# Moving the scatters of many-counted rows forward in the Pool queue of an argmax, gather and scatter kernel

## The chip, the cores and the metric

One core of a Trainium2 chip runs the whole kernel. The metric is the device time of one execution in microseconds (us). The profile's span is some 2 us shorter than the device time, because it starts and ends with the instructions.

## The reference, cut to what matters

```python
B, S, H = (8, 2048, 2560)
best_j = np.argmax(scores, axis=2)            # for each of 2048 rows of a batch, one chosen row
gathered = values[b_idx, best_j, :]
out = np.zeros_like(values)
np.add.at(out, (b_idx, best_j, slice(None)), gathered)
```

So an output row is zero if nobody chose it, a copy of the row of `values` if it was chosen once, and that row times its count if it was chosen more often. A row has 10,240 bytes.

## The kernel before

VectorE finds the argmax of each score row, matmuls count the choices, and three lists are made per batch: rows chosen once, never, and many times. The GpSimd (Pool) queue then moves the rows by indirect DMA, 128 rows ("a column") at a time; rows of a column that are not on its list are skipped.

- `copy_once(t)`: values to output in DRAM, the single rows of column t.
- `scatter(zrow, zi)`: zeros to the output.
- `gather` into one of six staging slots in SBUF, ScalarE multiplies by the count, `scatter` to the output. A slot can be filled again only when its scatter has landed.

```python
        def gathers():
            for k in range(MCAP):                     # 5 columns
                v = stage()                           # next of NV = 6 slots
                gather(v, mi[:, k:k + 1])
                nc.scalar.activation(out=v, in_=v, func=..., scale=mc[:, k:k + 1])
                staged.append(v)
                if rest:
                    copy_once(rest.pop(0))

        def zeros():
            for k in range(ZLAST if b == B - 1 else ZCAP):    # 12 or 7 columns
                scatter(zrow[:], zi[:, k:k + 1], free_running)
                if rest:
                    copy_once(rest.pop(0))

        if b == 0:
            zeros()
            # ... ten steps of the next batch's counting ...
            gathers()
        else:
            gathers()
            zeros()
        for k in range(MCAP):
            scatter(staged[k], mi[:, k:k + 1])
```

The rows of a column are spread over the 16 DMA engines, and by chance of the input some engines get fewer single rows than others. For the last batch, `level_engines` counts each engine's rows of the whole kernel and hands out the last 746 zero rows so that all engines come to nearly the same total: the lightest two engines get 76 zero rows each, the heaviest 20.

## Time and profile before

| | before |
|---|---|
| median of the first three runs | 840.63 us (839.85 to 841.81) |
| span of the profiled run | 838.4 us |
| DMA busy share, slices 1 to 39 of 40 | 0.9 or more in each |
| VectorE / Pool busy | 81% / 33% |
| rows moved by the Pool queue | 20,762, that is 212.6 MB |

The DMA row of the page says what bounds the kernel: 16 engines that are nearly never idle. In this view the last two columns are the mean busy share of the 16 DMA engines and GB/s.

```profile
632.00:637.00 5.00, 0.00 (x0) 0.00 (x0) 4.97 (x4) 0.00 (x0) 2.00 (x2) 1.00 0.94 377
696.00:701.00 5.00, 0.05 (x2) 0.00 (x0) 1.01 (x10) 0.00 (x0) 2.21 (x3) 1.00 0.94 383
760.00:764.00 4.00, 0.00 (x0) 0.00 (x0) 0.00 (x0) 0.00 (x0) 1.99 (x2) 1.00 0.98 405
```

Full is about 1.01 or 1.02 here, since a packet starts a few ns before the previous one ends.

### The profile page before, as it was taken

How to read it: one execution, taken by the hardware profiler on the slowest of the kernel's cores; microseconds unless marked ns; L12 is line 12 of the kernel's file. 1: busy time of each engine (PE TensorE's matmuls, PEld its weight loads, DVE VectorE, ACT ScalarE, POOL GpSimd, SP SyncE). 2: the span in 40 equal slices, each digit the busy share in tenths (PEclk: the TensorE clock that was granted, in tenths of full speed). 3: DMA queues.
4: the chain of work that ended last, by engine and by line, in shares of the span. 5: the costliest groups of instructions: out<-in, count | busy, mean ns of one | idle time of the engine just before them, and what ended most of it. 6: DMA issues, size and time to landing. Idle time of an engine off the chain costs nothing.

```text
span 838.4 us, 2053 instructions
## 1 busy us (share of the span) xinstructions
PE 14.7 (2%) x273; PEld 14.1 (2%) x273; DVE 678.6 (81%) x794; ACT 102.9 (12%) x43; POOL 274.3 (33%) x277
## 2 busy tenths in 40 slices
PE   0000000000000000000000000000000000000000
PEld 0000000000000000000000000000000000000000
DVE  7999999999999999999999999999999992000000
ACT  2000001401300002200003200013100500500500
POOL 0000743267101254130263300551305724734720
DMA  9999999999999999999999999999999999999992
GB/s 383 426 429 431 380 421 422 421 407 428 422 431 426 425 427 431 426 426 427 427 428 428 428 427 425 429 425 427 427 426 409 420 425 412 417 416 418 418 418 117
DMA packets 48111, 347.04 MB, mean 414 GB/s; under 512 B 19014, under 2 KB 19014, under 8 KB 19014
## 3 DMA queue, kind: packets, MB, share of 16 engines
q0 software_dynamic: 38736, 212.67, 61.4%
q1 hardware_dynamic: 9360, 134.22, 37.6%
q14 instruction: 13, 0.11, 0.0%
q8 instruction: 2, 0.03, 0.0%
HBM read 354.42 MB, written 300.15 MB: 781 GB/s over the span
## 4 chain that ended last, share of the span: by engine, by line
DVE 69%; DMA 12%; POOL 5%; issue 4%; another core or an unknown queue 4%; ACT 0%; PE 0%; POOLq 0%
DVE am L185 32%; DVE mx L184 29%; DMA out_dram<-vbig,many_i 9%; DMA vbig<-in_values_dram,many_i 3%; POOL out_dram L151 2%; DVE oh_lo L194 2%; POOL out_dram L33 2%; DVE oh L321 2%; POOL vbig L146 1%; DVE lo L190 1%; DMA vbig<-in_scores_dram 1%; DVE oh_hi L198 0%; ACT vbig L359 0%; DVE put L336 0%
## 5 line engine op out<-in xcount | busy, mean ns | idle before, releaser
L185 DVE FIND_INDEX8 am<-mx,s_tile 128x8 uint32<-128x2048 f32 x116 | 265.0, 2285 | 0.0
L184 DVE MAX8 mx<-s_tile 128x8 f32<-128x2048 f32 x116 | 264.3, 2278 | 0.0
L33 POOL DMA_INDIRECT out_dram<-in_values_dram,ones_i x128 | 131.2, 1025 | 157.1 <-DVE m L292 119.0
L359 ACT ACTIVATE vbig<-vbig,many_c 128x2560 f32<-128x2560 f32 x40 | 96.7, 2426 | 693.8 <-DMA vbig<-in_values_dram,many_i 693.8
L146 POOL DMA_INDIRECT vbig<-in_values_dram,many_i x40 | 42.4, 1060 | 230.2 <-DMA out_dram<-vbig,many_i 182.3
L151 POOL DMA_INDIRECT out_dram<-vbig,many_i x40 | 38.9, 972 | 122.5 <-ACT vbig L359 118.0
L151 POOL DMA_INDIRECT out_dram<-zrow,zero_i x61 | 60.6, 994 | 18.9 <-issue 18.9
L184 DVE MAX8 mx<-vbig 128x8 f32<-128x2048 f32 x12 | 27.4, 2279 | 4.8 <-DMA vbig<-in_scores_dram 4.8
L185 DVE FIND_INDEX8 am<-mx,vbig 128x8 uint32<-128x2048 f32 x12 | 27.4, 2285 | 0.0
L194 DVE TENSOR_TENSOR oh_lo<-lo,lane_f 128x512 bf16<-128x512 uint32 x32 | 22.2, 693 | 0.4
L321 DVE TENSOR_TENSOR oh<-lo,fill_f 128x2048 f16<-128x2048 uint32 x8 | 18.3, 2291 | 0.3
L203 PE MATMUL cnt_ps<-oh_hi,oh_lo 128*128 128x16 bf16 x128 | 8.1, 174 | 578.3 <-DVE oh_hi L198 578.3
L203 PEld LDWEIGHTS <-oh_lo 128*128 128x128 bf16 x128 | 8.4, 105 | 578.1 <-DVE oh_lo L194 577.1
L185 DVE MATCH_VALUE_LOAD am<-mx,s_tile 128x8 f32 x116 | 10.7, 92 | 4.0
L198 DVE TENSOR_TENSOR oh_hi<-hi,lane_f 128x64 bf16<-128x64 uint32 x32 | 6.9, 217 | 0.0
L190 DVE TENSOR_SCALAR lo<-am 128x4 uint32<-128x4 uint32 x32 | 5.8, 183 | 1.1
L339 PE MATMUL l_ps<-put,oh 128*128 128x32 f16 x128 | 4.7, 188 | 68.5 <-DVE put L336 68.5
L339 PEld LDWEIGHTS <-oh 128*128 128x128 f16 x128 | 4.6, 104 | 69.6 <-DVE oh L321 59.2
L192 DVE TENSOR_SCALAR hi<-am 128x4 uint32<-128x4 uint32 x32 | 5.5, 172 | 0.0
L326 DVE TENSOR_TENSOR ez<-hi,lane_f 128x256 f16<-128x256 uint32 x8 | 3.3, 418 | 0.0
L336 DVE TENSOR_TENSOR put<-ez,row_f 128x256 f16<-128x256 f16 x8 | 3.3, 417 | 0.0
L347 DVE TENSOR_SCALAR e<-l_ps 128x32 f32<-128x32 f32 x8 | 1.5, 185 | 2.0 <-PE l_ps L339 2.0
(91 smaller groups left out, 60.3 us busy)
## 6 DMA issues: line engine op xcount, KB each, us to landing
s_tile<-in_scores_dram SPq DMA_DIRECT2D x58, 2048.0 KB, 12.0
vbig<-in_scores_dram SPq DMA_DIRECT2D x5, 2048.0 KB, 32.6
vbig<-in_scores_dram SPq DMA_DIRECT2D x2, 1024.0 KB, 6.1
out_dram<-in_values_dram,ones_i POOLq DMA_INDIRECT x128, 28.3
out_dram<-zrow,zero_i POOLq DMA_INDIRECT x61, 25.4
vbig<-in_values_dram,many_i POOLq DMA_INDIRECT x40, 32.3
out_dram<-vbig,many_i POOLq DMA_INDIRECT x40, 46.4
```

The lines of the kernel that those rows point to most:

```text
L33: return eng.add_instruction(ins)
L146: nc.gpsimd.indirect_dma_start(out=v, out_offset=None, in_=values_flat[:, :], in_offset=bass.IndirectOffsetOnAxis(ap=idx, axis=0), bounds_ ...
L151: note(nc.gpsimd.indirect_dma_start(out=out_flat[:, :], out_offset=bass.IndirectOffsetOnAxis(ap=idx, axis=0), in_=v, in_offset=None, bound ...
L184: nc.vector.max(out=mx[:], in_=rows)
L185: nc.vector.max_index(out=am[:, g, :], in_max=mx[:], in_values=rows)
L190: nc.vector.tensor_single_scalar(out=lo[:], in_=am[:, :, 0], scalar=P - 1, op=ALU.bitwise_and)
L194: nc.vector.tensor_tensor(out=oh_lo[:], in0=lo[:].unsqueeze(2).to_broadcast([P, G, P]), in1=lane_f[:].unsqueeze(1).to_broadcast([P, G, P]) ...
L198: nc.vector.tensor_tensor(out=oh_hi[:], in0=hi[:].unsqueeze(2).to_broadcast([P, G, NT]), in1=lane_f[:, 0:NT].unsqueeze(1).to_broadcast([P, ...
L203: nc.tensor.matmul(out=cnt_ps[:], lhsT=oh_lo[:, g, :], rhs=oh_hi[:, g, :], start=(t == 0), stop=(t == NT - 1))
L321: nc.vector.tensor_tensor(out=oh[:], in0=lo[:].unsqueeze(2).to_broadcast([P, NT, P]), in1=fill_f[:].unsqueeze(1).to_broadcast([P, NT, P]), ...
L339: nc.tensor.matmul(out=l_ps[:], lhsT=oh[:, t, :], rhs=put[:, t, :], start=(t == 0), stop=(t == NT - 1))
L359: nc.scalar.activation(out=v, in_=v, func=mybir.ActivationFunctionType.Copy, bias=0.0, scale=mc[:, k:k + 1])
```

## The change

The intent: a batch's scatters go out earlier, so its staging slots come free earlier and the next batch's gathers wait less. No instruction is added or removed.

```diff
+    ZHEAD = 4
...
-        def zeros():
-            for k in range(ZLAST if b == B - 1 else ZCAP):
+        def zeros(columns):
+            for k in columns:
...
+        nz = ZLAST if b == B - 1 else ZCAP
         if b == 0:
-            zeros()
+            zeros(range(nz))
...
         else:
             gathers()
-            zeros()
+            zeros(range(ZHEAD))
         for k in range(MCAP):
             scatter(staged[k], mi[:, k:k + 1])
+        if b > 0:
+            zeros(range(ZHEAD, nz))
+        assert not rest
         yield
```

In batches 2 to 6 three zero columns and three copy columns go behind the scatters, in batch 7 eight and three. In batch 1 it is three and one, because that batch starts with six copy columns and not four.

## The prediction

> **What bounds the kernel now.** I read the page's second part (the 40 slices) first, then the DMA queues, the waits, the stretches of the tail, and last the Pool queue in order of time.
>
> ```profile
> span 838.4 us, 2053 instructions
> ...
> DVE  7999999999999999999999999999999992000000
> ...
> POOL 0000743267101254130263300551305724734720
> DMA  9999999999999999999999999999999999999992
> ...
> q0 software_dynamic: 38736, 212.67, 61.4%
> q1 hardware_dynamic: 9360, 134.22, 37.6%
> ```
>
> The DMA row is full in 39 of 40 slices, while Pool, the engine whose order changes, is busy a third of the time and VectorE has nothing left after about 697 us. q0 is the Pool queue (copies, zeros, gathers, scatters), q1 the score loads: 61.4 + 37.6 = 99% of the 16 engines' span. The chain of waits puts 69% on VectorE; I do not take that as the bound, since the same chain is then followed through DMA for its last 240 us and the DMA row has no hole under the VectorE part either.
>
> ```profile
> POOL vbig L146 <- DMA out_dram<-vbig,many_i: 182.3, 19, 41.5
> ...
> POOL out_dram L151 <- ACT vbig L359: 118.0, 25, 9.9
> ```
>
> These two waits (total, times, longest) are what the change acts on: a gather waits until the previous batch's scatter has left its staging slot, and a scatter waits until ScalarE has multiplied a gathered tile. They look large, 300 us, but Pool can wait as long as its queue still holds transfers. Whether it does is read from the stretches (the last two columns are DMA share and GB/s):
>
> ```profile
> 630.00:640.00 10.00, 0.00 (x0) 0.00 (x0) 9.93 (x7) 0.00 (x0) 4.17 (x5) 1.00 0.98 398
> 690.00:700.00 10.00, 0.59 (x16) 0.58 (x16) 6.11 (x25) 0.00 (x0) 1.51 (x2) 1.00 0.97 404
> 750.00:760.00 10.00, 0.00 (x0) 0.00 (x0) 0.00 (x0) 0.00 (x0) 0.00 (x0) 1.00 1.02 422
> 810.00:820.00 10.00, 0.00 (x0) 0.00 (x0) 0.00 (x0) 0.00 (x0) 0.00 (x0) 1.00 0.97 403
> 820.00:830.00 10.00, 0.00 (x0) 0.00 (x0) 0.00 (x0) 0.00 (x0) 0.00 (x0) 1.00 0.36 149
> ```
>
> From 750 to 760 Pool does nothing and DMA still moves 422 GB/s. After Pool's last issue (ends at 803.55 us) the transfers go on until about 829.6 in the packet records, then some 9 us of closing work follow. So the end is set by the bytes.
>
> **What the Trainium skill says.** "DMA: Bandwidth & Descriptors", section "Queues, rings and completion order": each of the 16 engines takes a ring's descriptors in order and goes round-robin between the queues. Its section "Anatomy of one DMA — SWDGE (gpsimd) path" says that DMA engines never wait on semaphores, the issuing sequencer does. Both agree with the trace: the gather issued at 770.59 landed at 795.06, 24 us behind older work. Section "Why a DMA increments its semaphore by 16 and not by 1": a transfer counts as landed when the slowest engine has; I use that for the tail. "Perfetto Trace Analysis", section "Per-instruction lifecycle": the profiled time of a Pool DMA is descriptor generation, not movement; the trace agrees, 0.96 us shown for a scatter against a median of 46.4 us to landing.
>
> **The change part by part.** It removes and adds no instruction. In batches 1 to 7 three zero columns (eight in the last batch) and three single-row copies go behind the five scatters. One issue takes 1.28 us (0.98 busy, 0.30 issue).
>
> Sizes: the reference's draw is fixed, so I counted rows. Over all batches 6131 are never chosen, 5875 once, 4378 more often; with gather and scatter that is 6131 + 5875 + 2 x 4378 = 20762 rows of 10,240 B = 212.6 MB, which is q0's size. Batch 7 has 746, 757 and 545. A full column (128 rows, 1.31 MB) takes 3.1 us at the tail's 418 GB/s; a copy column (47 rows) 1.15 us.
>
> *A middle boundary, batch 6 to 7, in the tail's rate.* The zeros start at 710.77. Now four zeros and four copies (8 x 1.28 = 10.2 us) end at 721.0, where the first scatter stands instead of at 728.73. Multiplies end at 717.25, 721.42, 725.67, 731.01 and 733.33, so the scatters go out near 721.0, 722.3, 726.0, 731.3 and 733.6, that is 7.7, 7.7, 5.3, 1.3 and 0.3 us earlier. Only the early ones gain; the last was bound by its gather. The six issues behind take Pool to 742.3. The transfers moved are 1.83 zero columns (5.7 us) and three copies (3.4 us), 9.1 us no longer ahead of the first scatter, which lands near 752 instead of 761. The first gather that reuses a slot then waits about 2 us where it waited 18.87:
>
> ```profile
> 741.56 0.99 POOL L33 DMA_INDIRECT out_dram<-in_values_dram,ones_i  x1 [0.30 <-issue]
> 761.43 1.01 POOL L146 DMA_INDIRECT vbig<-in_values_dram,many_i  x1 [18.87 <-DMA out_dram<-vbig,many_i]
> ```
>
> The columns are start, busy time, the instruction, and its idle time with the releaser. That is 17 us of Pool's time, and I expect next to nothing of it in the span: that gather still has all of batch 6 ahead of it in the same ring, in another order, so with a ring that never empties it lands when it landed before. What it can win is the dips: 630 to 640 moved 398 GB/s and 690 to 700 moved 404, against about 427 around them. That is 10 x 29/427 + 10 x 23/427 = 1.2 us in all. The moved columns lie just where these dips begin, so I count half to all: **-0.6 to -1.2 us**.
>
> *The last batch.* Gathers are issued by about 763, four zeros and their copies by 775. Its multiplies end where they ended:
>
> ```profile
> 792.40 2.43 ACT L359 ACTIVATE vbig<-vbig,many_c 128x2560 f32<-128x2560 f32 x1 [1.06 <-DMA vbig<-in_values_dram,many_i]
> 795.09 2.43 ACT L359 ACTIVATE vbig<-vbig,many_c 128x2560 f32<-128x2560 f32 x1 [0.27 <-DMA vbig<-in_values_dram,many_i]
> ```
>
> So Pool stands at the scatters from 775 until 797.5, where it waited 0.3 us before, and then issues eight zeros and three copies: 11 x 1.28 = 14.1 us, ending near 812.6 instead of 803.55. **Pool ends 9 us later.** Is that hidden? Behind the last gather, on the slowest engine at 795, still lie five copies and four zero columns, about 5.8 + 8 to 12 us, and four scatters of 3.1 us, over 26 us together; it reaches 821 without anything issued after 795. So the latest engine has no hole. The leveling of the last batch, worked out from the same counts, gives one engine 20 zero rows and the lightest 76. The lightest has almost no backlog at 775: nine columns issued there last it 18 us from 763, to about 781, and the scatters come to it at 783, 786.8, 791.4, 794.9 and 797.5 with 3.1 us each. It stands idle perhaps 3 to 5 us; then 44 zero rows and some 9 copied rows of 0.39 us take it to about 820, still ahead of the 829.6 of the latest. Cost **0, at worst +4 us**.
>
> Sum: 840.63 - 0.9 + about 0.3 for a small chance of the worst = **840.0 us**.
>
> **The rivals.** (1) *The early slot wins:* Pool's 182 us of slot waits shrink and the span with them. For it: Pool is at the end of the chain. Against it: DMA was full during those waits. Even if it won all dips and half of the uneven end (829.6 against some 822 if all engines ended together), that is 5 us: 835.5. (2) *A new wait takes its place:* Pool stands at the scatters (118 us of waits grow to perhaps 180) with nine issued columns behind the last gather instead of fifteen, the ring runs dry, and what is dry is lost. For it: after 618 us there are no score loads to fill in. Against it: 18 us of work are still behind the last gather. If it happened on the latest engine in the last two batches, some 5 us each: 850. (3) *Pool becomes the bound of the tail:* 14 us of issue for 10 us of rows (267 zero rows and 3 x 47 copies at 0.0245 us). Against it: the scatters' 13 us are still queued when it begins; perhaps +2 us.
>
> **Range and chances.** The median I expect is **840.0 us**, 8 times in 10 between **836.5** and **844.5**: the lower end is about four fifths of rival 1, the upper half of rival 2; runs of the kernel before already spread over 2 us. Over 2% would be 17 us. Faster by that is more than dips and uneven end hold together, chance **0.02**; slower needs the ring dry for 17 us, **0.03**; within 2% **0.95**.
>
> **What would show it.** Pool's slot waits fall well below 182 us, its waits for ScalarE rise well above 118, both without effect. DMA stays at 1.0 between 740 and 815; the dip near 635 is shallower. Pool's last issue falls near 812, its wait before the last batch's scatters sums to some 15 to 20 us. The multiplies of batch 7 still start near 780 to 795. I would be wrong if stretches with DMA share under 0.95 appeared before 810 (rival 2), or if the multiplies of batch 7 came several us earlier (rival 1).

## The result, and the profile after

| | before | after |
|---|---|---|
| median, six runs each | 840.62 us | 835.80 us (835.43 to 836.25) |
| ratio | | 0.9942 (0.9929 to 0.9955) |
| span | 838.4 us | 834.0 us |
| last row landed (packet records) | 829.65 us | 824.58 us |

Ratios here and below are the mean time of one kernel's runs over that of the other's in the same rounds, so they differ a little from the ratio of the medians. The change is 0.6% faster, and its 835.80 us lies just under the predicted 836.5 to 844.5.

The same rows of the page after:

```profile
span 834.0 us, 2053 instructions
...
POOL 0000642256021250071410422501516167266260
DMA  9999999999999999999999999999999999999993
...
q0 software_dynamic: 38736, 212.67, 61.5%
q1 hardware_dynamic: 9360, 134.22, 37.9%
```

The bytes are the same; 38,736 and 9,360 packets as before. The waits after (total, times, longest):

```profile
POOL out_dram L152 <- ACT vbig L360: 236.5, 39, 24.7
...
POOL vbig L147 <- DMA out_dram<-vbig,many_i: 83.6, 16, 21.1
```

Pool waits 99 us less for slots and 118 us more for multiplied tiles: it waits longer in all, and the kernel is faster. The sum of Pool's waits says nothing about the time. The stretches do:

```profile
632.00:637.00 5.00, 0.00 (x0) 0.00 (x0) 4.97 (x5) 0.00 (x0) 3.24 (x4) 1.00 1.02 420
696.00:701.00 5.00, 0.59 (x16) 0.48 (x15) 1.52 (x12) 0.00 (x0) 3.82 (x4) 1.00 1.01 422
...
820.00:830.00 10.00, 0.00 (x0) 0.00 (x0) 0.00 (x0) 0.00 (x0) 0.00 (x0) 1.00 0.15 51
```

Both dips are full again, and in 820 to 830 us the share is 0.15 where it was 0.36: the engines stop more nearly together. The Pool queue in order of time and ScalarE's last batch (start, busy, instruction, idle before it and releaser) show that the main times of the prediction came true:

```profile
752.13 1.01 POOL L147 DMA_INDIRECT vbig<-in_values_dram,many_i  x1 [1.97 <-DMA out_dram<-vbig,many_i]
...
781.70 0.98 POOL L152 DMA_INDIRECT out_dram<-vbig,many_i  x1 [7.67 <-ACT vbig L360]
785.52 0.97 POOL L152 DMA_INDIRECT out_dram<-vbig,many_i  x1 [2.84 <-ACT vbig L360]
...
810.33 0.96 POOL L152 DMA_INDIRECT out_dram<-zrow,zero_i  x1 [0.30 <-issue]
```

```profile
779.00 2.43 ACT L360 ACTIVATE vbig<-vbig,many_c 128x2560 f32<-128x2560 f32 x1 [45.53 <-DMA vbig<-in_values_dram,many_i]
```

The first reused slot was free at 752.13 after a wait of 1.97 us (predicted: 752, 2 us), Pool's last issue ended at 811.3 (predicted 812.6), and the last batch's multiplies began 1.5 us earlier. Not all of it fitted: Pool began the zeros of batch 6 at 701.59 and not at 710.77, because the boundary before it had changed too, and then stood 6.09 us at the first scatter. Yet the last row landed 5.1 us earlier.

**Which engines ended last.** The trace records each DMA packet with start, length and size, without its engine. On one engine a packet starts 3 to 4 ns before the previous ends, a row takes 385 ns and a skipped row appears as a 4-byte packet of 9 ns. Which rows each engine moves, in which order, follows from the reference's fixed input and from the spread of partitions over engines: for transfers from SBUF that of the Trainium skill, "DMA: Bandwidth & Descriptors", section "The descriptor swizzle", engine = 8 x (p >> 6) + ((p >> 2) & 7); for DRAM to DRAM p >> 3, as the kernel's own leveling assumes. I searched the packet records backwards for each engine's known sequence of rows and skips. Before, all 16 were found, over 220 or more consecutive packets each; after, 14. So this trace agrees with that page's mapping. The end of each engine's last packet, with its zero rows of the last batch:

```
engine (zero rows)   before    after
 0 (24)              819.2     818.8
 1 (21)              819.3     820.5
 3 (20)              825.7     824.2      <- heaviest
 4 (35)              824.7     824.2
11 (64)              827.1     820.5
 8 (59)              827.4     824.2
 9 (76)              829.6     823.7      <- lightest
12 (76)              829.6     824.6      <- lightest
```

Before, the **lightest** engines ended last, four microseconds behind the heaviest. The leveling gave them the most zero rows at the end in the belief that they had a lead; they had lost that lead earlier by standing idle, and by rows that took longer than the others (both below).

Linking the packets into 16 chains without any knowledge of the engine, and counting after 622 us: before, gaps of over 50 ns sum to 17.1 engine-us (microseconds summed over the engines), the two longest being 4.02 us (from 696.9) and 3.92 us (from 632.3), each on a single engine; after, the sum is 1.6 and the longest 0.30. This linking does not say whose gap it is, and where several engines stand at once it may pair ends and starts wrongly. Following the known sequences across the gaps does say it: engine 12 stood 3.8 us from 632.4, engine 11 3.2 us from 696.9, engine 9 3.8 us in three pieces near 635, 699 and 763, engine 8 1.0 us. These are the four that end last. Engines 0, 1, 7, 10, 13 and 15 have no gap; 4, 5 and 14 could not be followed all the way. Rows that took longer than 385 ns add 31.8 engine-us before and 2.5 after. The mean end of the 16 engines went from 823.2 to 820.9 us (2.3 us), the distance from there to the last from 6.5 to 3.7 us (2.8 us); together the 5.1 us.

From the last packet to the end of the span is a stretch of its own: 8.7 us before, 9.4 after, and 7.7 to 10.5 in the runs below, one profile each. No run shows what sets it, so differences of 1 us or so between runs are read below from the last packet too.

### The profile page after: what moved, and what is told of

Its sections match the earlier page's. It is cut to its first block, busy times and chain, and to the rows that moved or that the text cites. A ratio compares the mean times of both kernels' runs of the same rounds, so it can differ in the third digit from the quotient of the medians.

```text
span 834.0 us, 2053 instructions
## 1 busy us (share of the span) xinstructions
PE 14.7 (2%) x273; PEld 14.1 (2%) x273; DVE 679.2 (81%) x794; ACT 103.0 (12%) x43; POOL 272.8 (33%) x277
## 3 DMA queue, kind: packets, MB, share of 16 engines
q0 software_dynamic: 38736, 212.67, 61.5%
q1 hardware_dynamic: 9360, 134.22, 37.9%
## 4 chain that ended last, share of the span: by engine, by line
DVE 71%; issue 9%; DMA 9%; POOL 6%; another core or an unknown queue 2%; PE 0%; POOLq 0%
DVE am L186 32%; DVE mx L185 30%; DMA out_dram<-vbig,many_i 8%; POOL out_dram L33 3%; POOL out_dram L152 3%; DVE oh_lo L195 2%; DVE oh L322 2%; POOL vbig L147 1%; DMA vbig<-in_scores_dram 1%; DVE lo L191 1%; DVE oh_hi L199 0%; DVE hi L193 0%; DVE put L337 0%; DVE ez L327 0%
```

## The experiments

**Theory A.** Before, Pool waits for a slot until a scatter has landed on the slowest engine. (The wait that ended at 761.43 shows it: that scatter's last packet ended at 743.62 on engine 15, at 747.44 on engine 12 and at 760.83 on engine 3, the heaviest.) Behind the scatters only five copies and one gather are queued. The lightest engines finish those and stand idle for some 4 us, twice after 620 us, when no score loads fill in. The moved columns keep them fed. **Theory B:** the gain is made in the last batch, where zeros now end the queue. **Theory C:** each microsecond by which a slot comes free earlier counts.

All kernels were correct. "Before" is the kernel before in the same rounds.

| run | edit | before | this | ratio (95%) |
|---|---|---|---|---|
| mid_only | new order in batches 1 to 6 | 840.19 | 836.52 | 0.9961 (0.9947 to 0.9975) |
| last_only | in batch 7 | 840.19 | 838.97 | 0.9986 (0.9973 to 1.0) |
| three_only | in batches 4 to 6 | 840.19 | 835.30 | 0.9942 (0.9928 to 0.9955) |
| corr34 | old order, leveling cap 34 | 840.19 | 838.09 | 0.9976 (0.9962 to 0.9989) |
| head6_three | 4 to 6, behind the 6th zero column | 839.63 | 838.96 | 0.9986 (0.9973 to 0.9999) |
| head2_three | 4 to 6, behind the 2nd | 839.63 | 844.91 | 1.0064 (1.0051 to 1.0077) |
| nb6 | old order, 6 score buffers | 839.63 | 844.92 | 1.0061 (1.0048 to 1.0074) |
| nb6_nv7 | and 7 slots (confounded) | 839.63 | 867.95 | 1.0331 (1.0317 to 1.0344) |
| nb6_slot7 | 7 slots, mended | 839.71 | 840.11 | 1.0002 (0.9988 to 1.0015) |
| head5_three | 4 to 6, behind the 5th | 839.71 | 835.30 | 0.9945 (0.9931 to 0.9958) |
| early_mid | in batches 1 to 3 | 839.71 | 843.50 | 1.0041 (1.0028 to 1.0055) |
| late_all | in batches 4 to 7 | 839.71 | 834.65 | 0.9937 (0.9924 to 0.9951) |

### Where in the run the gain is made

The changed kernel, with the order chosen by batch:

```diff
+            head = ZHEAD if b < B - 1 else nz         # mid_only
+            head = ZHEAD if b == B - 1 else nz        # last_only
+            head = ZHEAD if 4 <= b <= 6 else nz       # three_only
+            head = ZHEAD if b <= 3 else nz            # early_mid
             gathers()
-            zeros(range(ZHEAD))
+            zeros(range(head))
```

> Only batches 1 to 6 have the new order; the last batch is as before. Theory A (the lightly loaded DMA engines run out of queued transfers while Pool waits for a staging slot, and the moved transfers keep them fed): nearly the whole gain, 835.5 to 837 us, and the DMA share is back at 1.0 in 630 to 640 and 690 to 700. Theory B (the gain is made in the last batch, by zeros that end the queue): 840 to 841 us.

> Only the last batch has the new order. Theory A: 840 to 841 us, the dips at 630 to 640 and 690 to 700 stay. Theory B: 835 to 837 us.

> Only batches 4, 5 and 6 have the new order. Theory A: as batches 1 to 6 together, 835.5 to 837 us, since until 618 us the score loads fill every engine, and only the slot waits of batches 5, 6 and 7 come after that or just before it. Rival: the gain comes from the Pool queue running ahead over many batches, then this keeps about half of it, 838 to 839 us.

> The new order in batches 1, 2 and 3 alone. Theory A: nothing, 839.5 to 841 us, with the dips at 630 to 640 and 690 to 700 as before, since the score loads keep all engines fed in that part. Rival (Pool runs ahead from early on): 838 us or less.

Batches 4, 5 and 6 alone give 0.58% less, as much as the whole change; batch 7 alone gives 0.14%, at the edge of its interval. (`three_only` is 0.2 us and `last_only` 1.0 us under what theory A expected.) Theory B falls, and so does the rival of a lead that builds up over many batches. The two stretches of `three_only` and of `last_only`, in that order:

```profile
630.00:640.00 10.00, 0.00 (x0) 0.00 (x0) 9.92 (x7) 0.00 (x0) 6.78 (x7) 1.00 1.02 421
690.00:700.00 10.00, 0.59 (x16) 0.58 (x16) 7.72 (x29) 0.00 (x0) 7.10 (x7) 1.00 1.01 418
```

```profile
630.00:640.00 10.00, 0.00 (x0) 0.00 (x0) 9.90 (x9) 0.00 (x0) 4.02 (x5) 1.00 0.99 397
690.00:700.00 10.00, 0.59 (x16) 0.58 (x16) 7.32 (x28) 0.00 (x0) 1.38 (x2) 1.00 0.97 404
```

The dips are gone with batches 4 to 6 and stay with batch 7. `early_mid` missed all expectations: it is 0.41% slower than before, and its second dip is deeper (8 us at share 0.88, where the kernel before has 0.97):

```profile
696.00:704.00 8.00, 0.34 (x13) 0.23 (x9) 1.01 (x10) 0.00 (x0) 2.88 (x3) 1.00 0.88 348
```

So the early batches are not neutral; by which path I did not settle. It is not that Pool meets the later slot waits at another time: the one before the first dip ends at 634.44 us, before at 634.18. And it is only in part the dip: the last packet landed 1.5 us later than before (831.19 against 829.65), and the stretch after it took 10.5 us in place of 8.7. `mid_only` (1 to 6) is 1.2 us behind `three_only` (the intervals overlap), but not by its transfers: its last packet landed earlier (823.99 against 824.68), and the stretch after it took 10.5 us against 9.3. Likewise less than half of what `last_only` gains is in its transfers (829.08 against 829.65).

### Which engines set the end

```diff
-    CORR = 56
+    CORR = 34
```

> The kernel before, with the cap on the last batch's extra zero rows at 34 in place of 56: the two lightest engines get 58 zero rows in place of 76, the heaviest 24 in place of 20. Theory A (the engines that end last in the kernel before are the lightest two, because they lost time dry): their end comes 18 x 0.385 = 6.9 us earlier, the heaviest engine ends 4 x 0.385 = 1.5 us later and is then among the last, near 827.2 in place of 829.6: 838 to 839.5 us. The prediction's view (the heaviest engine ends last and has no hole): 842 us, slower by 1.5.

0.24% faster than before, with the old order and the dips still there. Engines 9 and 12, now with 58 zero rows, ended at 822.1 and 822.8 us in place of 829.6, 7 us earlier as worked out; engine 8 (58) was last at 827.5, engine 3 (24) ended at 826.3, 0.6 us later where 1.5 was expected. Had the heaviest been last before, the time would have risen. It is the lightest that set the end.

### How much must lie behind the scatters

```diff
+            head = 6 if 4 <= b <= 6 else nz           # head6_three; 5 and 2 in the others
```

> As the run with batches 4, 5 and 6 alone, but the scatters stand after the sixth zero column: only one copy column and a nearly empty zero column go behind them, about 50 rows or 1.2 us of transfers in place of about 390 rows or 9.6 us. Theory A: a dry stretch shortens by the time of the transfers moved, so each of the two or three dry stretches of some 4 us on the lightest engines loses 1.2 us: 837.5 to 839 us. Rival: it is the place of the scatters ahead of the last zeros that matters, whatever is moved: 835.5 us.

> Batches 4 to 6 with the scatters after the fifth zero column: about 220 rows, 5.4 us of transfers, go behind them. Theory A: the dry stretches of some 4 us are just covered, 835 to 836.5 us. Rival (gain in proportion to what is moved, 9.6 us giving 4.9): 837.5 to 838 us.

> Batches 4, 5 and 6 with the scatters after the second zero column: about 740 rows or 18 us of transfers go behind them. Theory A: the dry stretches were 4 us and are gone at 9.6 us already, so nothing more is won: 834.8 to 836.5 us. Rival (each microsecond by which a slot comes free earlier counts): 830 to 832 us. If the wait for the multiplied tiles now runs the engines dry instead: 837 us or more.

With 1.2 us of transfers moved the gain is 0.14%, with 5.4 us 0.55%, with 9.6 us 0.58%. That saturates where the idle stretches of 4 us are covered; a gain in proportion, theory C, would have had 0.33% at 5.4 us. At 18 us the kernel is slower than before (its runs spread from 843.0 to 846.6; the trace is of the 843.0). Its Pool queue shows why:

```profile
718.43 0.98 POOL L152 DMA_INDIRECT out_dram<-vbig,many_i  x1 [12.88 <-ACT vbig L360]
722.59 0.97 POOL L152 DMA_INDIRECT out_dram<-vbig,many_i  x1 [3.19 <-ACT vbig L360]
726.84 0.97 POOL L152 DMA_INDIRECT out_dram<-vbig,many_i  x1 [3.28 <-ACT vbig L360]
732.19 0.97 POOL L152 DMA_INDIRECT out_dram<-vbig,many_i  x1 [4.38 <-ACT vbig L360]
```

```profile
728.00:736.00 8.00, 0.00 (x0) 0.00 (x0) 0.00 (x0) 4.75 (x2) 2.16 (x3) 1.00 0.90 379
```

Now only two zero and three copy columns lie between the last gather and the scatters; Pool stands at the scatters for the multiplied tiles, and in that wait the queue runs dry, at a share of 0.90. The new wait has taken the old one's place. Engines 9 and 12 are last again, at 831.6 and 830.3 us.

### The slot wait without any reordering

A seventh staging slot in the old order should do the same. It needs room, so the control has six score buffers.

```diff
-    NB = 7
+    NB = 6                          # nb6
-    NV = 6
+    NV = 7                          # nb6_nv7, and
-    NX = NV * H // (R * S)
+    NX = 3                          # nb6_slot7
```

> Control for the next run: the kernel before with six score buffers in place of seven. All theories: 840 to 842 us, as VectorE does not bound.

> The old order, six score buffers, seven staging slots in place of six: one more gather and copy are queued before Pool has to wait for a slot, some 4.3 us of transfers. Theory A: the dry stretches of some 4 us nearly vanish without any reordering, 836 to 838 us, 3 to 5 us under the control. Rival (the order itself makes the gain, not the slot wait): as the control.

> The extra staging slot again, with the first score loads kept to the same three tiles of the staging area as in the control with six score buffers (in the failed run a fourth tile made the score loads wait 126 us for the first scatters). Theory A: no dry stretch after 620 us, the lightest engines no longer last by 2 us and more, 1.2 to 5 us under the control's 844.9, so 840 to 843.5 us. Rival (the order itself makes the gain): 844.9 us and the dips of the control.

The control missed its expectation: with six buffers the score loads stall before Pool has its first list, and the DMA share is 0.59 for 8 us, where the kernel before has 1.00:

```profile
78.00:86.00 8.00, 0.25 (x4) 0.29 (x5) 7.44 (x15) 0.00 (x0) 0.00 (x0) 1.00 0.59 205
```

(That is 3.3 us of all engines, of the 5.3 us that the control lost; the rest is not accounted for. The dips near 640 and 704 are still there.) The first try with seven slots failed as an experiment: the staging area also holds the first score tiles, a seventh slot made room for a fourth tile, and the score loads then waited 126 us for the first scatters:

```profile
SPq L177 <- DMA out_dram<-vbig,many_i: 125.9, 1, 125.9
```

Mended, with three such tiles as in the control, seven slots take 840.11 us: 4.8 us under the control of the call before, or 0.6% when each is set against the kernel before of its own rounds (1.0002 against 1.0061). The order is the old one and the gain is that of the reordering. It had the control's loss at 80 us (share 0.63), but no dip near 640 and hardly one near 704:

```profile
640.00:650.00 10.00, 0.26 (x4) 0.26 (x4) 9.90 (x11) 0.00 (x0) 7.70 (x8) 1.00 1.02 421
...
700.00:710.00 10.00, 0.00 (x0) 0.00 (x0) 0.00 (x0) 0.00 (x0) 4.01 (x4) 1.00 1.01 418
```

The control's lines for the same stretches have 1.00 and 409, and 0.96 and 392. Linked as above, single engines' gaps after 622 us sum to about 3 engine-us in place of the control's 17, and the last engine ends 3.9 us after the mean one in place of 6.6, much as the reordering made it 3.7 in place of 6.5.

### The best version

> The new order in batches 4 to 7: the run with batches 4 to 6 (835.3) and the run with the last batch (1.2 us under before) put together. If both parts add: 834 us. If the last batch's part was only what the dry engines had left over: as the run with 4 to 6, 835 to 836 us.

```diff
+            head = ZHEAD if b >= 4 else nz
```

834.65 us, the fastest median of all and 0.63% under before. Its interval overlaps that of the changed kernel (0.9942), so it beats the kernel before clearly and the changed one not for certain. The last batch's own part did not add in full: 0.63% against 0.58% and 0.14%. Of the 0.65 us to `three_only`'s 835.30, a difference inside the intervals, the profiles give 0.4 to the last packet (824.32 against 824.68).

## Why the prediction was wrong

**Right.** DMA bounds the kernel; Pool's slot waits fall (182 to 84 us) and its waits for ScalarE rise (118 to 237 us); at the boundary from batch 6 to 7 the first scatter lands and the slot wait shrinks as computed, though Pool comes to it 9 us earlier; in the last batch Pool stands at the scatters for 18.4 us in sum (predicted 15 to 20), its last issue moves to 811.3 us, and no engine runs dry from that (the gaps after sum to 1.6 engine-us from 622 us on). The term "at worst +4 us" for the last batch did not come up, nor did the 3 to 5 us for which the lightest engine was to stand idle there.

**Wrong, step one: the size of the dips.** "That is 10 x 29/427 + 10 x 23/427 = 1.2 us in all. The moved columns lie just where these dips begin, so I count half to all: -0.6 to -1.2 us." This divides the lost time by 16. The lost time lay on few engines, up to 4 us at a stretch on one, and the end of the kernel is the end of the last engine and not of the mean one. The mean end moved by 2.3 us, already twice the term, since the rows that took longer than 385 ns cost more ((31.8 - 2.5) / 16 = 1.8 us) than the gaps did ((17.1 - 1.6) / 16 = 1.0 us; together 0.5 us more than the mean end moved, which stays open); the rest came from the last engines. It was this term that was mis-sized: about -5 where I had -0.9.

**Wrong, step two: who is last.** "So the latest engine has no hole." I took the latest engine for the heaviest, and the lightest for being at 820 us, "still ahead of the 829.6 of the latest". The trace shows the lightest two at 829.6 and the heaviest at 825.7, and `corr34` shows it by experiment. An engine that the leveling had made up to the common total can end last only if it has lost time; I had the leveling's 20 and 76 rows in hand and asked only what the new order would cost the light engines, not what the old one cost them.

Rival 1 had the time nearly right (835.5), by winning "all dips and half of the uneven end". It was set aside with "DMA was full during those waits", which is true of the mean share from 750 to 760 us and not of single engines near 634 and 698. Its own reason, that Pool is at the end of the chain, is not what the runs showed: after the change Pool waited 20 us longer in all, and the kernel was faster.

One reading in the prediction is stronger than its line: the 24 us from 770.59 to 795.06 fit the order within a ring, but say nothing of the turn between the queues, which this argument does not need.

**Open.** Why the new order in batches 1 to 3 alone costs 0.41%, and what sets the 7.7 to 10.5 us after the last packet. And the slow rows: from 622 us on their sum is large in the profiles with dips (31.8 engine-us before, 27.3 in `corr34`, 24.0 in `last_only`) and small where the dips are gone (2.5 after, 2.9 in `mid_only`, 3.4 in `late_all`), so there they go with the dips, but no run shows what makes such a row slow.

## What to carry to other kernels

Where several DMA engines share the work and the work is leveled over the whole run, ask at every wait on a landed transfer how long the engine with the least queued can go on, since the wait lasts until the one with the most has landed. A mean share of 0.94 for 5 us may be 4 us lost on the engine that ends the kernel. Put work that waits for nothing behind the transfers that somebody will wait for, just enough to cover the stretch (5 us did here), and leave enough ahead of them to cover the other wait: with 18 us moved, the gain became a loss.

## What the Trainium skill lacked or had wrong

- "Perfetto Trace Analysis", section "Identifying the Most-Contended Engine", calls occupancy misleading for the 16 DMA engines and sends the reader to bandwidth. Here both means hid the loss alike: 0.94 and 377 GB/s over 5 us, where single engines stood still for up to 4 us. The page does name single DMA engines as a possible bound and speaks of a track for each, but the packet records here carry no engine, and for these it has no way to tell the engines apart; the 3 to 4 ns by which packets overlap, with the known row pattern, did it.
- "DMA: Bandwidth & Descriptors" has no figure for a skipped row of an indirect transfer: a 4-byte packet of 9 ns here, against 385 ns for a row of 10,240 bytes.
- The same page, section "Latency and other measured facts", says that engines 7 and 15 are usually slower. Not seen here: from 622 us on, their rows beyond 385 ns add 0.8 us (engine 7) and 2.1 us (engine 15), where the others that could be followed have 0.5 to 4.2 us. (Engine 15 also ended first, at 815.4 us, but the leveling gave it 15 rows, or 5.8 us, less than the common 1299.)
- The page tells that a transfer has landed only when all engines are done, but not what follows for a queue that levels unequal shares: about 5 us of 840 in this kernel.
